# Expert rows added by accumulating scatters onto the base rows and a second tensor, instead of plain scatters into two planes

## The chip, the core and the metric

The kernel runs on one core of a Trainium2 chip. The metric is the device time of one execution in microseconds. A core has TensorE (PE, matmuls), VectorE (DVE), ScalarE (ACT), GpSimd (POOL) and SyncE (SP). SP issues the plain DMAs here, POOL the indirect ones, and 16 DMA engines move the bytes of both.

## What is computed

One layer of a hybrid model on 512 rows of 1024 numbers in f32: a layer norm, a gated delta rule and a differential attention in parallel, a second layer norm, and then a mixture of 16 experts in 4 groups. The change is in that last part:

```
group_prob = softmax(h @ w_rg + b_rg);  g_val, g_idx = top_k(group_prob, 1)
e_prob = softmax(the 4 expert logits of that group);  e_val, e_idx = top_k(e_prob, 2)
e_w = e_val / sum(e_val) * g_val                      # two experts of each row
hid = silu(h @ w_gate[e]) * (h @ w_up[e])             # 1024 -> 256
ffn = sum over the row's two experts of e_w * (hid @ w_down[e])   # 256 -> 1024
ple = sigmoid(h @ w_ple_gate + b) * (p @ w_ple_proj)
out = layer_norm(alpha * h + ffn + ple, ln2_g, ln2_b)
```

## The kernel before

Rows are worked on in four tiles of 128. The part ahead of the experts is long and untouched but for the router. It leaves in DRAM `h1d`, the rows that go into the experts, and `acc`, the base rows (alpha * h plus the ple term, scaled).

**Routing** (`route`, `slots`). `R` holds for each row and each of its two choices one-hot expert, row number and weight. `slots` turns it, with one-hot matmuls, into three tables with a column for each expert: `ts` (which row stands in slot p of the expert, an index out of bounds where the slot is empty), `tw` (its weight) and `td` (twice the row number, plus one where the expert is the row's second choice).

**Experts** (the loop at L1422). For expert e, POOL gathers its rows from `h1d` three experts ahead (L1223), TensorE transposes them (`psx`), `up` makes the gate and up products, `down` the down product, and ScalarE writes the weighted rows to `y` (L1288, two buffers). An indirect DMA of POOL then scatters `y` into `planes` (L1291), a tensor of 2 x 512 rows that was cleared at the start of the kernel (`clear_planes`, L324): each pair of row and choice has its own plane row, so nothing is added in DRAM. Matmuls are made of three products of split operands, and the splits are written by ScalarE (the high part, L265) and VectorE (the low part, L266).

**Weights** come on SP's queue (`load_to`, L246): for each expert two loads `wE` and one `wD`, 1 MB each. From the first expert on, a load waits until the load three before it has landed (`DEEP`, "few loads in flight").

**The last two experts** (14 and 15, `LAST`) aren't scattered: `keep_expert` keeps their weighted rows in SBUF (`ykeep`, high and low part, L1283 and L1284), and `spread` puts them on their rows with one-hot matmuls (`plast`, L1479).

**The end** (`finish`). Base rows are loaded to `at` (L1340) and planes to `pl` (L1345, 1 MB a tile). VectorE adds the planes of tiles 0 to 2 (`add_plane`, L1349, two a tile), TensorE adds those of tile 3 by identity matmuls (L1476). `add_last` adds `plast` and sums the rows (L1486, L1488), ScalarE takes the squares (L1489), `dev` and POOL's power make the deviation (L1492, L209), `norm` scales the rows (L1496), TensorE transposes them (`pzt`), and ScalarE and VectorE write the output pieces (L1518, L1520), which SP stores.

**What sets the order.** Queues are in order. A scheduler orders instructions of the traced program by their dependencies; `strict` keeps the order of writing on an engine within its block, and `behind` puts instructions behind the last one of an engine. A DMA on a DRAM tensor waits for earlier DMAs on the same tensor whose rows may be the same; an indirect one counts as touching all rows. `beyond` works on rows past 128 of an expert, behind a branch.

Of the kernel before, what the change touches and what calls it, by code (L numbers as in the profile page):

```python
# [12 lines left out]
I32 = mybir.dt.int32  # L13
# [59 lines left out]
def block_kernel(ctx, tc, x, pT, wA, wB, wO, wM, wPG, wPP, wE, wD, cols, rows, consts, out):  # L73
# [242 lines left out]
    planes = dp.tile([2 * S, D], F32, name="planes")  # L316
# [3 lines left out]
    def clear_planes():  # L320

        dst = planes.rearrange("(p r) (a b) -> p (r a) b", r=8, b=512)
        for i in range(4):
            nc.sync.dma_start(dst[:, 4 * i:4 * i + 4, :],  # L324
                              nil.rearrange("p (o b) -> p o b", o=1).to_broadcast([128, 4, 512]))
# [770 lines left out]
    def route():  # L1096
# [50 lines left out]
        R = cp.tile([128, 8, 64], F32, name="Rr")  # L1147
        POOL.memset(R[:, 0:4, 48:64], 0.0)
# [7 lines left out]
        DVE.tensor_copy(R[:, 4:8, 48:64], R[:, 4:8, 32:48])  # L1156
# [29 lines left out]
        RT["s"], RT["w"], RT["d"] = slots(0)  # L1186


    def slots(b):
# [5 lines left out]
        for c in range(8):  # L1195
            oh = sp.tile([128, 128], F32, name="oh", tag="oh")
            DVE.tensor_scalar(oh, iota, pos[:, c:c + 1], None, op0=OP.is_equal)
            PE.matmul(pi[:, 0:64], oh, RT["R"][:, c, :], start=c == 0, stop=c == 7)
# [77 lines left out]
    def down(hT, dw, wcol, idxs, mmul, keep=None, y=None, inside=None):  # L1276
# [53 lines left out]
    def finish_expert(e):  # L1330
        down(hTs.pop(e), weights("D", e, loads=ahead(e), splits=SPLITS), ecol("w", e), ecol("d", e), mm3)
# [10 lines left out]
    def load_planes(*tiles):  # L1342
        for t in tiles:
            pl[t] = big([2, 1024], name="pl")
            nc.sync.dma_start(pl[t].rearrange("p c d -> p (c d)"),  # L1345
                              planes[t * 256:(t + 1) * 256, :].rearrange("(p c) d -> p (c d)", c=2))

    def add_plane(t, c):
        DVE.tensor_tensor(at[t // 2][:, t % 2, :], at[t // 2][:, t % 2, :], pl[t][:, c, :], op=OP.add)  # L1349

    def add_planes(*tiles):
        for t in tiles:
            for c in range(2):
                add_plane(t, c)
# [291 lines left out]
```

## Time and profile before

| | |
|---|---|
| median of 3 runs | 671.49 us (670.57 to 672.28) |
| profiled execution | 671.27 us, of which the span is 669.5 us |
| TensorE busy | 650.7 us, 97% of the span |
| VectorE busy | 496.0 us, 74% |
| ScalarE busy | 371.8 us, 56% |
| moved by DMA | 127.17 MB, 190 GB/s in the mean |
| granted TensorE clock | 1.00 to 640 us, 0.87 in the mean from 640 to 670 us |

Times in rows are microseconds from the span's start. A row of a time line gives start, busy time, engine, line, operation, and in brackets how long the engine had been idle and what ended it. SPq and POOLq are the queues that issue DMAs. "out<-in" names the tiles with their numbers left out.

### The profile page before, as it was taken

Reading aid. Unit: us, or ns where it says so; the run is one execution under the profiler, and the core shown is the slowest. Engines: PE = TensorE matmul, PEld = TensorE weight load, DVE = VectorE, ACT = ScalarE, POOL = GpSimd, SP = SyncE. Lnnn points to the kernel's source line nnn. Section 1 sums busy time; section 2 is a strip of 40 time slices with the busy share of each in tenths; the row PEclk is TensorE's granted clock in tenths of the full one; section 3 lists DMA queues with packets and bytes.
Section 4 is the critical chain, followed back from the end, with each engine's and each line's share of the span. In section 5 each row is a group of like instructions: output and inputs, shape, how many; then the busy total and the mean of one; then the engine's idle time right before and its main releaser. Section 6 shows DMA issues by size and latency. Waiting matters only on the chain.

```text
span 669.5 us, 9576 instructions
## 1 busy us (share of the span) xinstructions
PE 650.7 (97%) x3515; PEld 544.3 (81%) x3516; DVE 496.0 (74%) x922; ACT 371.8 (56%) x694; POOL 93.8 (14%) x108
## 2 busy tenths in 40 slices
PE   8999999999998999999999999999999999999993
PEld 4998888888887888888888888899978888888762
DVE  4956678995367684864726284879789999999984
ACT  6707544562466564564523232123379888989734
POOL 2000030100001212200000010200213122221310
PEclk9999999999999999999999999999999999999997
DMA  8994015113103410231611464195489999999553
GB/s 314 404 411 176 1 21 199 63 64 95 64 1 134 141 64 1 69 120 64 251 64 64 137 269 165 64 367 198 162 317 397 378 368 357 359 373 341 187 242 130
DMA packets 31764, 127.17 MB, mean 190 GB/s; under 512 B 9585, under 2 KB 11249, under 8 KB 20576
## 3 DMA queue, kind: packets, MB, share of 16 engines
q1 hardware_dynamic: 27392, 118.73, 47.2%
q0 software_dynamic: 4320, 7.77, 3.2%
q8 instruction: 29, 0.48, 0.3%
q14 instruction: 23, 0.19, 0.1%
HBM read 111.91 MB, written 22.54 MB: 201 GB/s over the span
## 4 chain that ended last, share of the span: by engine, by line
PE 58%; DVE 5%; ACT 3%; issue 1%; POOL 0%; POOLq 0%; ACTq 0%
PE pg L291 12%; PE pg L290 12%; PE pg L289 12%; PE pup L291 3%; PE pup L289 3%; PE pup L290 3%; PE pdn L291 2%; PE pdn L290 2%; PE pdn L289 2%; PE psx L1232 2%; ACT sE L265 1%; PE pov L931 1%; DVE sE L266 1%; DVE sD L266 1%; PE psc L902 1%; ACT xT L1234 1%
## 5 line engine op out<-in xcount | busy, mean ns | idle before, releaser
L289 PE MATMUL pg<-hTh,sA 128*128 128x512 f32 x320 | 129.6, 405 | 0.0
L291 PE MATMUL pg<-hTh,sA 128*128 128x512 f32 x320 | 126.8, 396 | 0.0
L290 PE MATMUL pg<-hTl,sA 128*128 128x512 f32 x320 | 126.5, 395 | 0.0
L266 DVE TENSOR_TENSOR sE<-wE,sE 128x1024 fp32r<-128x1024 f32 x64 | 75.4, 1219 | 0.3 <-ACT sE L265 0.3
L291 PEld LDWEIGHTS pg<-hTh,sA 128*128 128x128 f32 x320 | 60.2, 188 | 13.2
L289 PEld LDWEIGHTS pg<-hTh,sA 128*128 128x128 f32 x320 | 60.3, 188 | 11.5
L290 PEld LDWEIGHTS pg<-hTl,sA 128*128 128x128 f32 x320 | 60.3, 189 | 11.2
L265 ACT ACTIVATE sE<-wE 128x1024 fp32r<-128x1024 f32 x64 | 64.5, 1070 | 0.5 <-PE pg L291 0.4
L265 ACT ACTIVATE sA<-wA 128x1024 fp32r<-128x1024 f32 x40 | 41.4, 1055 | 34.7 <-PE pg L291 31.9
L266 DVE TENSOR_TENSOR sA<-wA,sA 128x1024 fp32r<-128x1024 f32 x40 | 48.7, 1225 | 6.8 <-ACT sA L265 6.6
L289 PE MATMUL pup<-sE,xT 128*128 128x512 f32 x128 | 51.6, 403 | 0.0
L290 PE MATMUL pup<-sE,xT 128*128 128x512 f32 x128 | 50.4, 394 | 0.7 <-DVE sE L266 0.7
L291 PE MATMUL pup<-sE,xT 128*128 128x512 f32 x128 | 50.4, 394 | 0.0
L266 DVE TENSOR_TENSOR sD<-wD,sD 128x1024 fp32r<-128x1024 f32 x32 | 37.8, 1220 | 3.5 <-ACT sD L265 3.3
L290 PE MATMUL pg<-sPG,H1H 128*128 128x262 f32 (+1 forms) x128 | 36.6, 286 | 0.0
L289 PE MATMUL pg<-sPG,H1H 128*128 128x262 f32 (+1 forms) x128 | 36.5, 286 | 0.0
L291 PE MATMUL pg<-sPG,H1L 128*128 128x262 f32 (+1 forms) x128 | 36.5, 285 | 0.0
L265 ACT ACTIVATE sD<-wD 128x1024 fp32r<-128x1024 f32 x32 | 32.5, 1081 | 0.0
L906 ACT ACTIVATE tt<-tt,mn 128x128 f32<-128x128 f32 (+3 forms) x32 | 17.8, 556 | 24.1 <-DVE mn L904 24.0
L1223 POOL DMA_INDIRECT xr<-h1d,ts x16 | 19.1, 1194 | 85.0 <-PE psx L1232 39.9
L530 DVE SCALAR_TENSOR_TENSOR acc<-pad,col,acc 128x512 f32<-128x512 f32 x36 | 26.7, 742 | 3.8 <-ACT acc L528 3.5
L290 PEld LDWEIGHTS pup<-sE,xT 128*128 128x128 f32 x128 | 24.1, 188 | 6.1 <-DVE sE L266 1.2
(369 smaller groups left out, 1528.2 us busy)
## 6 DMA issues: line engine op xcount, KB each, us to landing
wE<-wE SPq DMA_DIRECT2D x32, 1024.0 KB, 9.8
wA<-wA SPq DMA_DIRECT2D x20, 1024.0 KB, 5.0
wD<-wD SPq DMA_DIRECT2D x16, 1024.0 KB, 10.0
wPG<-wPG SPq DMA_DIRECT2D x4, 1048.0 KB, 7.0
planes<-nil SPq DMA_DIRECT2D x4, 1024.0 KB, 11.2
wO<-wO SPq DMA_DIRECT2D x4, 1024.0 KB, 4.8
wM<-wM SPq DMA_DIRECT2D x4, 1024.0 KB, 4.8
pl<-planes SPq DMA_DIRECT2D x4, 1024.0 KB, 10.9
```

What stands on the lines that cost most here:

```text
L265: ACT.activation(hl[:, 0], r, AF.Copy)
L266: lo_eng.tensor_tensor(hl[:, 1], r, hl[:, 0].bitcast(F32), op=OP.subtract)
L289: PE.matmul(ps, lh, rh, start=i == 0, stop=False)
L290: PE.matmul(ps, lh, rl, start=False, stop=False)
L291: PE.matmul(ps, ll, rh, start=False, stop=i == n - 1)
L530: DVE.scalar_tensor_tensor(acc, pad[:, j:j + 512], w[j], acc, op0=OP.mult, op1=OP.add)
L902: PE.matmul(ps[:, :n], qs[:, tq], kl[:, :n], start=False, stop=True)
L906: ACT.activation(tt[:, :n], tt[:, :n], AF.Exp, bias=mn[:, m:m + 1], scale=-1.0, accum_out=(s0[:, qt:qt + 1] if m == 0 else s1))
L931: PE.matmul(po[:, qt * 128:(qt + 1) * 128], aT[:, k * 128:(k + 1) * 128], VB[:, k, vo:vo + 128], start=k == 0, stop=k == qt)
L1223: POOL.indirect_dma_start(out=xr, out_offset=None, in_=h1d, in_offset=bass.IndirectOffsetOnAxis(ap=idx, axis=0), bounds_check=S - 1, oob_i ...
L1232: PE.transpose(ps[:, k * 128:(k + 1) * 128], xr[:, (kk * 4 + k) * 128:(kk * 4 + k + 1) * 128], ident)
L1234: ACT.activation(xT[:, 0, ks, :], h4(ps), AF.Copy)
```

## The change

The planes become one tensor `odd` of 512 rows, cleared at the start by two transfers instead of four. The scatter of an expert adds to its destination (`compute_op=OP.add`): even experts add to `acc`, odd ones to `odd`, at the row number `ts`; the table `td` and what makes it go. The scatters of the loop now alternate between two tensors. At the end `at` is loaded from `acc` behind its scatters, `pl` from `odd` (0.5 MB a tile), and there is one addition a tile, all on VectorE. The additions are at new places: tile 0 ahead of the first `ykeep`, tiles 1 and 2 inside `keep_expert` of experts 14 and 15, tile 3 behind `add_last(0)`. Tile 0's norm goes to ScalarE (`slide`, `norm_act`), `norm(2)` stands ahead of the transposes, and the output pieces are divided otherwise between the two engines.

```diff
--- before.py
+++ after.py
...
-    planes = dp.tile([2 * S, D], F32, name="planes")
+    odd = dp.tile([S, D], F32, name="odd")
...
-        dst = planes.rearrange("(p r) (a b) -> p (r a) b", r=8, b=512)
-        for i in range(4):
+        dst = odd.rearrange("(p r) (a b) -> p (r a) b", r=4, b=512)
+        for i in range(2):
...
-        R = cp.tile([128, 8, 64], F32, name="Rr")
-        POOL.memset(R[:, 0:4, 48:64], 0.0)
+        R = cp.tile([128, 8, 48], F32, name="Rr")
...
-        DVE.tensor_copy(R[:, 4:8, 48:64], R[:, 4:8, 32:48])
...
-            PE.matmul(pi[:, 0:64], oh, RT["R"][:, c, :], start=c == 0, stop=c == 7)
+            PE.matmul(pi[:, 0:48], oh, RT["R"][:, c, :], start=c == 0, stop=c == 7)
...
-        td = cp.tile([128, 16], F32, name=nm("td"))
-        DVE.scalar_tensor_tensor(td, tf, 2.0, pi[:, 48:64], op0=OP.mult, op1=OP.add)
-        td_ = cp.tile([128, 16], I32, name=nm("tdi"))
-        DVE.tensor_copy(td_, td)
-        return ts_, tw, td_
+        return ts_, tw
...
-        POOL.indirect_dma_start(out=planes, out_offset=bass.IndirectOffsetOnAxis(ap=idxs, axis=0), in_=y, in_offset=None,
-                                bounds_check=2 * S - 1, oob_is_err=False)
+        POOL.indirect_dma_start(out=onto, out_offset=bass.IndirectOffsetOnAxis(ap=idxs, axis=0), in_=y, in_offset=None,
+                                bounds_check=S - 1, oob_is_err=False, compute_op=OP.add)
...
-        down(hTs.pop(e), weights("D", e, loads=ahead(e), splits=SPLITS), ecol("w", e), ecol("d", e), mm3)
+        down(hTs.pop(e), weights("D", e, loads=ahead(e), splits=SPLITS), ecol("w", e), ecol("s", e), mm3,
+             onto=(acc, odd)[e % 2])
...
+    def load_planes():
+        pl.update({i: big([2, 1024], name="pl") for i in range(2)})
+        for t in range(NT):
+            nc.sync.dma_start(pl[t // 2][:, t % 2, :], odd[t * 128:(t + 1) * 128, :])
+
+    def add_plane(t):
+        DVE.tensor_tensor(at[t // 2][:, t % 2, :], at[t // 2][:, t % 2, :], pl[t // 2][:, t % 2, :], op=OP.add)
...
         if e == NE - 1:
-            load_planes(2, 3)
             turn_last = late.pop(e)
 
             def between():
                 turn_last()
-                with behind(DVE):
-                    add_plane(0, 0)
-
-            keep_expert(e - 1, inside=between)
+                add_plane(1)
+
+            with behind(DVE), strict(DVE):
+                add_plane(0)
+                keep_expert(e - 1, inside=between)
+                keep_expert(e, inside=partial(add_plane, 2))
...
             load_base()
-            load_planes(0, 1)
-    keep_expert(NE - 1, inside=next_plane)
-    with behind(DVE):
-        add_planes(1)
+            load_planes()
...
-                if t == 3 and add:
-                    for c in range(2):
-                        PE.matmul(ps[-1], ident, pl[t][:, c, nh * 512:(nh + 1) * 512], start=c == 0, stop=False)
...
+        def slide(t):
+            DVE.tensor_tensor(st[t][:, 6:7], st[t][:, 2:3], st[t][:, 5:6], op=OP.mult)
+
+        def norm_act(t):
+            ACT.activation(R_[t], R_[t], AF.Identity, bias=st[t][:, 6:7], scale=st[t][:, 5:6])
...
             s0, s1, s2, s3 = (spread(t) for t in range(NT))
+            with behind(DVE):
+                add_last(0, s0)
             if add:
-                with behind(DVE):
-                    add_planes(2)
-            add_last(0, s0)
+                add_plane(3)
             add_last(1, s1)
             dev(0)
             add_last(2, s2)
-            norm(0)
+            slide(0)
             dev(1)
+            norm_act(0)
             add_last(3, s3)
             norm(1)
             dev(2)
+            norm(2)
             b0, b1 = [], []
             turn(0, b0)
             turn(1, b0)
-            norm(2)
             leave(0, b0, "AAAA", (4, 8))
...
-            leave(0, b0, "....AAVV", (4, 8))
-            leave(1, b1, "VAVVAVAV", (4, 8))
+            leave(0, b0, "....VAVV", (4, 8))
+            leave(1, b1, "AVAVAVAV", (4, 8))
```

On POOL the last scatters before, with the one-hot rows of the kept experts behind them (`y` is the expert's rows, `tdi` the integer table `td`):

```order
L1291 DMA planes<-y_5709,tdi_4344 1024x1024
L1291 DMA planes<-y_5806,tdi_4344 1024x1024
L1291 DMA planes<-y_5881,tdi_4344 1024x1024
L1291 DMA planes<-y_5928,tdi_4344 1024x1024
L1359 TENSOR_SCALAR to_row_5966<-cst,tf_4337 128x128 x4
```

and now:

```order
L1284 DMA acc<-y_5701,ts_4336 512x1024
L1284 DMA odd<-y_5798,ts_4336 512x1024
L1284 DMA acc<-y_5873,ts_4336 512x1024
L1284 DMA odd<-y_5920,ts_4336 512x1024
L1347 TENSOR_SCALAR to_row_5958<-cst,tf_4333 128x128 x4
```

The place in the queue is the same; the destination alternates, so that a scatter shares its tensor with the last but one.

On SP the end of the weight loads and the loads of the last part before:

```order
L246 DMA wD_5838<-wD 128x2048
L1340 DMA at_5991<-acc 128x1024 x2
L1340 DMA at_5992<-acc 128x1024 x2
L1345 DMA pl_5997<-planes 128x2048
L1345 DMA pl_5999<-planes 128x2048
L1345 DMA pl_6077<-planes 128x2048
L1345 DMA pl_6079<-planes 128x2048
```

and now:

```order
L246 DMA wD_5830<-wD 128x2048
L1334 DMA at_5983<-acc 128x1024 x2
L1334 DMA at_5984<-acc 128x1024 x2
L1339 DMA pl_5989<-odd 128x1024 x2
L1339 DMA pl_5990<-odd 128x1024 x2
```

The order stands. The loads of `acc` now come behind scatters into `acc` (the last is expert 12's) and those of `odd` behind expert 13's; half as much is loaded to `pl`.

On VectorE the end before, from the last expert's gate (`eth`) to the first sums of `add_last` (L1486):

```order
L1263 TENSOR_TENSOR eth_6073<-eth_6073,pup_6036 128x256
L1284 SCALAR_TENSOR_TENSOR ykeep_6081<-pdn_6082,tw_4335,ykeep_6081 128x512
L1273 TENSOR_TENSOR hT_6094<-psf_6091,hT_6094 128x256
L1349 TENSOR_TENSOR at_5991<-at_5991,pl_5997 128x1024
L1284 SCALAR_TENSOR_TENSOR ykeep_6081<-pdn_6098,tw_4335,ykeep_6081 128x512
L1284 SCALAR_TENSOR_TENSOR ykeep_6107<-pdn_6108,tw_4335,ykeep_6107 128x512
L1349 TENSOR_TENSOR at_5991<-at_5991,pl_5997 128x1024
L1284 SCALAR_TENSOR_TENSOR ykeep_6107<-pdn_6118,tw_4335,ykeep_6107 128x512
L1349 TENSOR_TENSOR at_5991<-at_5991,pl_5999 128x1024 x2
L1349 TENSOR_TENSOR at_5992<-at_5992,pl_6077 128x1024 x2
L1486 ISA at_5991,st_6129<-plast_6136,at_5991 128x512
```

and now:

```order
L1256 TENSOR_TENSOR eth_6067<-eth_6067,pup_6030 128x256
L1342 TENSOR_TENSOR at_5983<-at_5983,pl_5989 128x1024
L1277 SCALAR_TENSOR_TENSOR ykeep_6072<-pdn_6073,tw_4331,ykeep_6072 128x512
L1266 TENSOR_TENSOR hT_6085<-psf_6082,hT_6085 128x256
L1342 TENSOR_TENSOR at_5983<-at_5983,pl_5989 128x1024
L1277 SCALAR_TENSOR_TENSOR ykeep_6072<-pdn_6089,tw_4331,ykeep_6072 128x512
L1277 SCALAR_TENSOR_TENSOR ykeep_6098<-pdn_6099,tw_4331,ykeep_6098 128x512
L1342 TENSOR_TENSOR at_5984<-at_5984,pl_5990 128x1024
L1277 SCALAR_TENSOR_TENSOR ykeep_6098<-pdn_6109,tw_4331,ykeep_6098 128x512
L1463 ISA at_5983,st_6118<-plast_6125,at_5983 128x512
```

The first addition now stands ahead of the first `ykeep`, and the sums of `add_last` follow the last `ykeep` at once.

## Rows read from the trace of the kernel before

**Rows 1.** The page: busy time of the engines, and TensorE in 40 slices of the span, in tenths.

```profile
PE 650.7 (97%) x3515; PEld 544.3 (81%) x3516; DVE 496.0 (74%) x922; ACT 371.8 (56%) x694; POOL 93.8 (14%) x108
...
PE   8999999999998999999999999999999999999993
```

**Rows 2.** Who TensorE waited for from 480 to 645 us: the longest sum (us in total, times, longest).

```profile
PE pdn L289 <- ACT sD L265: 0.8, 1, 0.8
```

**Rows 3.** The chain of work that ended last, TensorE's transposes of the rows of two experts, nine apart (start, us).

```profile
511.49 0.87 PE psx L1232 x8
...
596.53 0.87 PE psx L1232 x8
```

**Rows 4.** What SP's queue waited for from 500 to 616 us (us in total, times, longest).

```profile
SPq L246 <- DMA wE<-wE: 68.8, 23, 4.1
SPq L246 <- DMA wD<-wD: 32.2, 12, 3.7
```

**Rows 5.** The time line of SP's queue: the pairs of loads of experts 8 and 14, the last two down weights, and the base rows.

```profile
533.31 3.38 SPq L246 DMA_DIRECT2D wE<-wE  x2
...
593.60 4.02 SPq L246 DMA_DIRECT2D wE<-wE  x2
...
610.60 3.71 SPq L246 DMA_DIRECT2D wD<-wD  x2
618.22 2.04 SPq L1340 DMA_DIRECT2D at<-acc  x4
```

**Rows 6.** Two lines of the code in one stretch each: the last load of weights, and the loads of the base rows, with the time from issue to landing.

```profile
L246 SPq DMA_DIRECT2D wD<-wD x1: 327/327/327, 614.0 to 614.0; - x1
...
DMA to landing us min/median/max: 9.2/9.2/9.2
...
L1340 SPq DMA_DIRECT2D at<-acc x4: 320/376/432, 618.2 to 619.8; - x4
...
DMA to landing us min/median/max: 6.2/7.4/8.9
```

**Rows 7.** The time line of ScalarE: the second half of expert 12's rows, the splits of the last two down weights, and the first operation behind them.

```profile
618.23 0.69 ACT L1288 ACTIVATE y<-pdn,tw 128x512 f32<-128x512 f32 x1 [0.71 <-PE pdn L291]
...
628.03 2.04 ACT L265 ACTIVATE sD<-wD 128x1024 fp32r<-128x1024 f32 x2
...
630.29 2.00 ACT L265 ACTIVATE sD<-wD 128x1024 fp32r<-128x1024 f32 x2
634.10 0.38 ACT L1271 ACTIVATE hT<-psf 128x256 fp32r<-128x256 f32 x1 [1.81 <-PE psf L1268]
```

**Rows 8.** The time line of VectorE at the end: gate of the last expert, first and last `ykeep`, plane additions, one `norm`, one `dev`, the last `norm`, output pieces.

```profile
637.07 0.42 DVE L1263 TENSOR_TENSOR eth<-eth,pup 128x256 f32<-128x256 f32 x1
638.32 0.75 DVE L1284 SCALAR_TENSOR_TENSOR ykeep<-pdn,tw,ykeep 128x512 fp32r<-128x512 f32 x1 [0.83 <-ACT ykeep L1283]
...
643.22 0.74 DVE L1284 SCALAR_TENSOR_TENSOR ykeep<-pdn,tw,ykeep 128x512 fp32r<-128x512 f32 x1
643.88 4.87 DVE L1349 TENSOR_TENSOR at<-at,pl 128x1024 f32<-128x1024 f32 x4
...
653.13 0.80 DVE L1496 TENSOR_SCALAR at<-at,st 128x1024 f32<-128x1024 f32 x1
653.85 0.15 DVE L1492 TENSOR_SCALAR st<-st 128x1 f32<-128x1 f32 x1
...
658.44 0.81 DVE L1496 TENSOR_SCALAR at<-at,st 128x1024 f32<-128x1024 f32 x1 [0.66 <-POOL st L209]
659.17 2.35 DVE L1520 TENSOR_SCALAR z<-pzt,col 128x256 f32<-128x256 f32 x5
661.71 1.00 DVE L1520 TENSOR_SCALAR z<-pzt,col 128x256 f32<-128x256 f32 x2 [0.19 <-ACT z L1518]
```

**Rows 9.** Busy time by stretch: stretch, its length, then PE, PEld, DVE, ACT and POOL, the granted clock, the busy share of the 16 DMA engines, and GB/s. The stretches are the router and first experts, one at the start in which only plain DMAs run, two among the experts, and one in which the last scatter runs nearly alone.

```profile
420.00:520.00 100.00, 98.98 (x661) 89.70 (x660) 86.66 (x198) 47.41 (x73) 18.59 (x13) 1.00 0.68 256
...
40.00:50.00 10.00, 10.00 (x84) 9.91 (x83) 3.25 (x9) 1.40 (x4) 0.00 (x0) 1.00 1.05 412
510.00:520.00 10.00, 10.00 (x50) 8.22 (x49) 10.00 (x13) 9.01 (x13) 2.74 (x2) 1.00 1.00 404
540.00:550.00 10.00, 10.00 (x54) 8.32 (x52) 9.63 (x12) 9.08 (x14) 2.17 (x2) 1.00 0.91 343
632.50:633.10 0.60, 0.60 (x5) 0.41 (x3) 0.60 (x2) 0.00 (x0) 0.60 (x1) 1.00 0.28 109
```

**Rows 10.** The time line of POOL: the last three scatters (experts 11 to 13). Then, for the scatters' line, the time from issue to landing over all 14.

```profile
614.12 0.99 POOL L1291 DMA_INDIRECT planes<-y,tdi  x1 [8.48 <-ACT sE L265]
623.58 0.97 POOL L1291 DMA_INDIRECT planes<-y,tdi  x1 [8.47 <-ACT sE L265]
630.39 1.02 POOL L1291 DMA_INDIRECT planes<-y,tdi  x1 [5.84 <-ACT eth L1261]
...
DMA to landing us min/median/max: 3.7/8.7/9.9
```

**Rows 11.** The page: POOL's DMA queue (packets, MB, share of 16 engines), and the indirect DMAs (count, us to landing).

```profile
q0 software_dynamic: 4320, 7.77, 3.2%
...
xr<-h1d,ts POOLq DMA_INDIRECT x16, 8.5
planes<-y,tdi POOLq DMA_INDIRECT x14, 8.7
```

More of the change, by code (lines that the diff above doesn't have):

```diff
@@ L1185, in route @@
         yield 1
-        RT["s"], RT["w"], RT["d"] = slots(0)
+        RT["s"], RT["w"] = slots(0)
     def slots(b):
@@ L1274, in turn_h, with down @@
         return hT
-    def down(hT, dw, wcol, idxs, mmul, keep=None, y=None, inside=None):
+    def down(hT, dw, wcol, idxs, mmul, keep=None, y=None, inside=None, onto=None):
         y = half_slot("y") if keep is None and y is None else y
@@ L1340, in load_base @@
             nc.sync.dma_start(at[t // 2][:, t % 2, :], acc[t * 128:(t + 1) * 128, :])
[L1342 to L1352, printed above, removed]
-            for c in range(2):
-                add_plane(t, c)
+    def load_planes():
[4 more added lines that the diff above has]
+        DVE.tensor_tensor(at[t // 2][:, t % 2, :], at[t // 2][:, t % 2, :], pl[t // 2][:, t % 2, :], op=OP.add)
     def find_rows(e):
@@ L1376, in beyond @@
             wd = dp.tile([3, 128, 16], F32, name="ovw")
-            dd = dp.tile([3, 128, 16], I32, name="ovd")
             for b in range(1, 4):
-                ts_, tw, td = slots(b)
+                ts_, tw = slots(b)
                 nc.sync.dma_start(sd[b - 1], ts_)
                 nc.sync.dma_start(wd[b - 1], tw)
-                nc.sync.dma_start(dd[b - 1], td)
             we = [big([4, 512], name="we") for _ in range(2)]
@@ L1386, in beyond @@
             y = half_slot("y")
-            is_, iw, id_ = tiny(1, "is", I32), tiny(1, "iw"), tiny(1, "id", I32)
+            is_, iw = tiny(1, "is", I32), tiny(1, "iw")
             with tc.For_i(0, NE, 1) as e:
@@ L1393, in beyond @@
                         nc.sync.dma_start(iw, wd[b - 1, :, bass.ds(e, 1)])
-                        nc.sync.dma_start(id_, dd[b - 1, :, bass.ds(e, 1)])
                         for kh in range(2):
@@ L1400, in beyond @@
                         turn_h(th, False, hT)
-                        down(hT, lambda f, sl: (wd_[:, f, sl], None), iw, id_, mm1, y=y)
+                        down(hT, lambda f, sl: (wd_[:, f, sl], None), iw, is_, mm1, y=y, onto=acc)
             load_base()
-            load_planes(*range(NT))
-            add_planes(*range(NT))
+            load_planes()
+            for t in range(NT):
+                add_plane(t)
             finish(False)
@@ L1416, in turn_into @@
             hTs[e] = turn_h(th, True)
-    def next_plane():
-        with behind(DVE):
-            add_plane(0, 1)
     for e in range(NE):
@@ L1457, in block_kernel @@
             load_base()
-            load_planes(0, 1)
-    keep_expert(NE - 1, inside=next_plane)
-    with behind(DVE):
-        add_planes(1)
+            load_planes()
     def finish(add=True):
@@ L1473, in spread @@
                 ps.append((gbank if 2 * t + nh in (4, 5, 6) else bank)("plast"))
-                if t == 3 and add:
-                    for c in range(2):
-                        PE.matmul(ps[-1], ident, pl[t][:, c, nh * 512:(nh + 1) * 512], start=c == 0, stop=False)
                 for e in LAST:
@@ L1479, in spread @@
                         PE.matmul(ps[-1], to_row[e][:, t, :], ykeep[e][:, i, nh * 512:(nh + 1) * 512],
-                                  start=e == LAST[0] and i == 0 and not (t == 3 and add), stop=e == LAST[1] and i == 1)
+                                  start=e == LAST[0] and i == 0, stop=e == LAST[1] and i == 1)
             return ps
@@ L1526, in finish @@
             s0, s1, s2, s3 = (spread(t) for t in range(NT))
+            with behind(DVE):
+                add_last(0, s0)
             if add:
-                with behind(DVE):
-                    add_planes(2)
-            add_last(0, s0)
+                add_plane(3)
             add_last(1, s1)
```

## The prediction

> **What bounds the kernel now.** I read the page first, then the waits of the stretch in which the experts run, then the time lines of its queues, and last the end of the kernel. TensorE is busy for 97% of the span, and the slices show it at 9 tenths in all but the first and the last [rows 1]. In the stretch of the experts it waits for almost nothing: the largest sum is one wait of 0.8 us, for a split weight [rows 2]. One expert takes (596.53 - 511.49)/9 = 9.45 us, read from the rows' transposes that open each [rows 3]. So TensorE sets the pace there, but a second engine runs beside it with less air than that suggests. The DMA queue of SP, which loads the weights, spends 68.8 + 32.2 = 101 us of the 116 us from 500 to 616 waiting for an earlier load to land [rows 4]: three loads are in flight at any time, and none of that waiting is for a free buffer. The load of expert 8's first half was issued at 533.31 and that of expert 14's at 593.60, so weights come at (593.60 - 533.31)/6 = 10.05 us an expert [rows 5], slower than the 9.45 us at which they are used. The kernel lives on the lead that the first loads have. At the end it is nearly gone: the last down weights, issued at 613.99, land 9.2 us later, at 623.2 [rows 6], and ScalarE starts to split them at 630.29 [rows 7]. The cover is 7.1 us, and 1.8 us more of idle ScalarE stands behind that split, before 634.10 [rows 7].
>
> The last part is another regime. From 637 on, VectorE is the chain: behind the last expert's second half (643.22) it adds four plane tiles in 4.87 us from 643.88, and then works on through the adds and norms until the last norm at 658.44, with gaps of no more than 0.7 us [rows 8].
>
> **What the end gains.** Before, six plane tiles are added on VectorE, four of them behind the last `ykeep`, and two more by identity matmuls. Now there are four tiles: one in front of the first `ykeep`, one inside each of the two kept experts, and one between `add_last(0)` and `add_last(1)`. Of the four behind the last `ykeep` three go: 3 x 4.87/4 = 3.65 us [rows 8]; the adds that stand earlier fill waits for ScalarE, 0.8 us and more [rows 8]. The identity matmuls cost nothing before, as TensorE was ahead of VectorE there, and give nothing. `norm(0)` (0.80 us) goes to ScalarE and leaves one 128x1 operation, 0.15 us like `dev` [rows 8]: VectorE gains 0.6 us, but ScalarE does the 1024 columns (1.0 us, as half of its sD pair [rows 7]) before the squares of tile 3, which `norm(3)` waits for; I keep 0.35 us. VectorE has seven output pieces behind `norm(3)` before and after, so nothing changes there. Sum: 4.0 us earlier, if all inputs are there in time.
>
> **What costs nothing.** One copy, one scalar-tensor-tensor and one cast fewer in the router, a memset less, matmuls of 48 columns for 64 and a few rows in another order: TensorE is busy 98.98 of 100 us there [rows 9], and at most its 1.0 us of idling could go. Half of the clearing (2 of 4 MB) goes from 30 to 50 us; TensorE is busy for every microsecond of that stretch too [rows 9], so the freed transfer hides behind it. The scatters' waits become looser. Before, each waits for the one before to land; the starts at 614.12, 623.58 and 630.39, 7 to 9.5 us apart, with a median landing of 8.7 us, are that chain [rows 10]. Now each waits for the last but one, some 19 us back. POOL's next row gather stands behind it, and the longest wait of TensorE, for a split, is 0.8 us [rows 2], so this gives nothing by itself; scatter 12 can start when its rows are written, near 619 [rows 7], and not at 623.58.
>
> **What accumulating costs.** No accumulating transfer is in this trace. What a plain indirect one costs the loads can be read. Loads alone run at 412 GB/s [rows 9], so three of 1.049 MB take 7.64 us. They take 10.05 us where one gather and one scatter an expert run beside them, so the two cost 2.41 us, 1.2 us each. By bytes it should be half: queue 0 moved 7.77 MB in 30 transfers [rows 11], 0.26 MB each, 0.63 us at 412 GB/s. The reason is seen where a scatter runs nearly alone (632.5 to 633.1): the 16 DMA engines are busy to a share of 0.28, four to five of them [rows 9]. Some 64 of 128 rows are real, they stand in the first partitions, and a part of the engines carries them, while a load has landed only when its slowest part has. The slices agree: 404 GB/s in 510 to 520, 343 GB/s in 540 to 550 [rows 9].
>
> An accumulating scatter must read its destination rows and write them. Lower bound of the extra: 0, if the read hides behind the write; less than a plain scatter is excluded, as it writes the same bytes. Upper bound: 2.4 us, a gather and a scatter's worth on top, if reading, adding and writing don't overlap. I take the read as what the nearest row has, a gather of as many rows: x = 1.2 us a scatter.
>
> The Trainium skill (Collectives: The Full Stack, "The bandwidth ceiling: the fold count and why AG ≠ RS ≠ AR") says that a DMA engine that adds has two sources to read in one ring, and got 32.35 GB/s where copying got 62.28. By that ratio, 1.93, the extra would be 0.93 x 1.2 = 1.1 us, an estimate, and the sum below 674.5 us; no accumulating transfer here shows it.
>
> Before the last down weights land there are 13 scatters (0 to 11, and now 12). 13 x 1.2 = 15.6 us, so they land at 623.2 + 15.6 = 638.8 us. That uses up the cover of 7.1 + 1.8 us; TensorE would be 6.7 us late. It isn't the last word. The base rows can now be loaded only when scatter 12 has landed, behind these weights, not at 618.22 [rows 5], and the odd rows behind them in the same queue. The four base loads ended 8.9 us after 619.8 [rows 6], at 628.7, 5.5 us behind the weights' landing; one of 0.5 MB takes about 1.4 us. So the first odd tile lands 5.6 + 1.4 = 7.0 us after the weights: 645.8 us. `add_plane(0)` is now ahead of the first `ykeep` on VectorE, a place reached at 637.5 before [rows 8]; behind it are queued both `ykeep`s, `hT` of the last expert, for which TensorE waits, and all of the end. So 645.8 - 637.5 = 8.3 us late, which contains TensorE's 6.7.
>
> Sum: +8.3 - 4.0 = +4.3 us on the profiled execution's 671.27 us. That stands 0.2 us under the median of the runs, 671.49. Forecast: 675.8 us. In general the change is -4.0 + max(0, 13x - 7.3) us: it breaks even at x = 0.87 us.
>
> **Rivals.** Faster, on the other side: the read of the destination hides. One mechanism, the place is the weight queue from 507 to 623 us, the price is x. Below x = 0.56 nothing of the lead is missed and the end's 4.0 us stand: 667.5 us; up to 0.72 it is still faster by 0.3%. For it: half of the DMA engines have air [rows 9], and the lead is 7.1 us. Against it: the loads wait for the slow half, and the end is no better if the odd rows come late.
>
> In between: x from 0.72 to 1.02 us, lead and gain cancel within 2 us: 671.5 us.
>
> Dearer: read, add and write in turn, x = 2.4. The lead is gone some experts earlier and each expert then takes over 12 us (10.05 + 2.4): -4.0 + 31.2 - 7.3 = +19.9, 691.4 us. For it: the loaded landing is 8.7 us against 3.7 us without load [rows 10], so this queue suffers from company. Against it: a DMA that reads one row while it writes another is what the plain ones do.
>
> **How the numbers follow.** 0.3% is 2.0 us, about what a measurement of this kernel can tell from no change. x above 1.02 us has 0.51 (0.40 up to x = 1.6, 681.0 us; 0.11 above), between 0.72 and 1.02 it has 0.14, below 0.35. So slower 0.51, same 0.14, faster 0.35. The likeliest case alone spans 673.5 to 681.0 us. The range takes in the faster case with 1.2 us of error in the end's sum, 666.3, and reaches up to x = 1.7, 682.0; it leaves out about 0.09 above and 0.08 below.
>
> **What would show it.** Right: weight loads of experts 8 to 14 issued 11 us apart or more, TensorE waiting for splits or splits for landings from expert 11 or 12 on, the last down weights landing near 639 us, VectorE waiting some microseconds before its first plane add, and 4 us fewer from there to the end. Wrong: loads still 10 us apart and no wait of ScalarE for one; then x is near 0, the end's gain is all there is, and the time is near 667.5. Spans of 12 us an expert would show the dear case. If the end from the first `ykeep` on isn't shorter by 3 to 5 us, the other term is wrong.

## The result, and the profile after

The changed kernel takes **680.71 us** (median of 4 runs, 679.96 to 683.27); the kernel before took 671.38 us beside it (4 runs, 670.57 to 672.28). The ratio is 1.0145, 95% interval 1.0114 to 1.0177: 9.3 us slower. The forecast was 675.8 us. The direction came as forecast, the size did not: 9.3 us where 4.3 were forecast. The profiled execution below is the longest of its four, 683.27 us with a span of 681.5; its own difference to the profiled one of before is 12.0 us, and sums read from it are held against 12.0, not against 9.3.

The page first. POOL's queue, which carries the gathers and scatters, moves the bytes it moved before [rows 11] in half as much time again, and waits for DMA are now a good part of the chain that ended last:

```profile
PE 653.1 (96%) x3507; PEld 548.8 (81%) x3508; DVE 493.6 (72%) x917; ACT 373.8 (55%) x695; POOL 101.1 (15%) x107
...
q0 software_dynamic: 4320, 7.78, 4.7%
...
PE 42%; DMA 22%; DVE 2%; issue 2%; ACT 1%; POOL 0%; SPq 0%; POOLq 0%; DVEq 0%; ACTq 0%
```

That chain before:

```profile
PE 58%; DVE 5%; ACT 3%; issue 1%; POOL 0%; POOLq 0%; ACTq 0%
```

4.7% of 681.5 us is 32.0 us of all 16 engines; before, it was 3.2% of 669.5, 21.4 us. The 14 scatters thus cost 10.6 us more, 0.76 us each over 16 engines, or 1.5 us each if half of the engines carry them. The whole queue's mean before was 21.4/30 = 0.71 us a transfer, 1.43 on half of the engines. If a plain scatter costs that mean, an accumulating one costs about twice as much.

The time line of SP's queue, to be read beside [rows 5] (start, us, engine, line, tiles, count):

```profile
537.45 4.14 SPq L246 DMA_DIRECT2D wE<-wE  x2
...
611.16 4.40 SPq L246 DMA_DIRECT2D wE<-wE  x2
...
629.32 2.80 SPq L246 DMA_DIRECT2D wD<-wD  x2
639.71 1.89 SPq L1334 DMA_DIRECT2D at<-acc  x4
```

The loads of experts 8 and 14 are now (611.16 - 537.45)/6 = 12.29 us an expert apart; they were 10.05, and TensorE uses an expert's weights up in 9.45. The lead is lost at expert 10: the split of its second half, on ScalarE's time line, is the first of 15 that wait for a load, and from there on most do. Then follows who ScalarE and TensorE waited for from 480 to 660 us (us in total, times, longest; the first two of these rows are ScalarE's, the others TensorE's):

```profile
580.90 2.01 ACT L265 ACTIVATE sE<-wE 128x1024 fp32r<-128x1024 f32 x2 [1.32 <-DMA wE<-wE]
```

```profile
ACT sE L265 <- DMA wE<-wE: 10.1, 10, 1.5
...
ACT sD L265 <- DMA wD<-wD: 3.6, 5, 1.1
...
PE psf L1261 <- DVE eth L1256: 9.7, 6, 2.1
PE pdn L289 <- DVE ykeep L1277: 2.0, 1, 2.0
```

Before, TensorE's longest sum was 0.8 us [rows 2], and ScalarE waited for no load. What these waits add up to is read at the last down weights, on ScalarE's time line, where [rows 7] had 630.29. The first `ykeep` stands beside it, first before, then, behind the split, now:

```profile
637.60 0.69 ACT L1283 ACTIVATE ykeep<-pdn,tw 128x512 fp32r<-128x512 f32 x1 [1.02 <-PE pdn L291]
```

```profile
642.26 2.00 ACT L265 ACTIVATE sD<-wD 128x1024 fp32r<-128x1024 f32 x2 [0.21 <-DMA wD<-wD]
...
649.09 0.69 ACT L1276 ACTIVATE ykeep<-pdn,tw 128x512 fp32r<-128x512 f32 x1 [1.00 <-PE pdn L291]
```

The split starts 12.0 us late and has just waited for its load, so that load landed at about 642.2, 19.0 us later than before (623.2). TensorE's product, which ScalarE copies as the first `ykeep`, is 11.5 us late. Last, VectorE at the end, beside [rows 8]:

```profile
651.16 1.22 DVE L1342 TENSOR_TENSOR at<-at,pl 128x1024 f32<-128x1024 f32 x1 [2.17 <-DMA pl<-odd]
652.31 0.74 DVE L1277 SCALAR_TENSOR_TENSOR ykeep<-pdn,tw,ykeep 128x512 fp32r<-128x512 f32 x1
...
657.98 0.74 DVE L1277 SCALAR_TENSOR_TENSOR ykeep<-pdn,tw,ykeep 128x512 fp32r<-128x512 f32 x1
658.64 0.68 DVE L1463 CUSTOM_DVE_ANT_0 at<-plast,at 128x512 f32<-128x512 f32 x1
...
668.99 0.81 DVE L1479 TENSOR_SCALAR at<-at,st 128x1024 f32<-128x1024 f32 x1 [0.66 <-POOL st L209]
```

The first plane add waits for the odd rows and starts 13.7 us later than VectorE reached that place before (637.5). From the last `ykeep` to the last `norm` it is now 11.0 us; it was 15.2 (643.22 to 658.44). But the last `ykeep` is 14.8 us late, 3.3 us more than the first on ScalarE. Between the two TensorE waited 2.0 us for VectorE's first `ykeep`, which stands behind the add that waits for the odd rows (the last row of the waits above). Then its clock fell, as the stretches show (columns of [rows 9]), first the kernel before, then two of the changed one:

```profile
654.00:656.00 2.00, 1.08 (x8) 0.84 (x8) 1.96 (x6) 1.00 (x3) 0.55 (x1) 1.00 0.01 4
```

```profile
646.00:648.00 2.00, 2.00 (x11) 1.61 (x10) 0.49 (x2) 0.29 (x1) 2.00 (x4) 1.00 0.86 272
654.00:656.00 2.00, 2.00 (x6) 1.60 (x5) 1.18 (x2) 0.54 (x1) 0.00 (x0) 0.50 0.01 4
```

A granted clock of 0.50 is the lower of its two levels: six matmuls fall into 2 us where eleven did just before.

### The profile page after: what moved, and what is told of

The parts are those of the page before. It is cut to its first block, busy times and chain, and to the rows that moved or that the text cites. A ratio compares the mean times of both kernels' runs of the same rounds, so it can differ in the third digit from the quotient of the medians.

```text
span 681.5 us, 9548 instructions
## 1 busy us (share of the span) xinstructions
PE 653.1 (96%) x3507; PEld 548.8 (81%) x3508; DVE 493.6 (72%) x917; ACT 373.8 (55%) x695; POOL 101.1 (15%) x107
## 4 chain that ended last, share of the span: by engine, by line
PE 42%; DMA 22%; DVE 2%; issue 2%; ACT 1%; POOL 0%; SPq 0%; POOLq 0%; DVEq 0%; ACTq 0%
DMA wE<-wE 18%; PE pg L289 12%; PE pg L291 12%; PE pg L290 12%; DMA odd<-y,ts 3%; PE pov L931 1%; DMA pl<-odd 1%; PE psc L902 1%; PE psc L901 1%; PE pzt L1488 1%; PE pat L919 1%; DVE at L1463 1%; PE psh L388 1%; DVE at L1342 0%; DVE z L1503 0%
## 5 line engine op out<-in xcount | busy, mean ns | idle before, releaser
L265 ACT ACTIVATE sE<-wE 128x1024 fp32r<-128x1024 f32 x64 | 64.6, 1064 | 11.2 <-DMA wE<-wE 10.1
L289 PEld LDWEIGHTS pg<-hTh,sA 128*128 128x128 f32 x320 | 60.4, 189 | 11.4
L290 PEld LDWEIGHTS pg<-hTl,sA 128*128 128x128 f32 x320 | 60.4, 189 | 11.1
L289 PE MATMUL pup<-sE,xT 128*128 128x512 f32 x128 | 52.3, 409 | 0.0
L290 PE MATMUL pup<-sE,xT 128*128 128x512 f32 x128 | 51.2, 400 | 0.7 <-DVE sE L266 0.7
L291 PE MATMUL pup<-sE,xT 128*128 128x512 f32 x128 | 51.0, 398 | 0.0
## 6 DMA issues: line engine op xcount, KB each, us to landing
wE<-wE SPq DMA_DIRECT2D x32, 1024.0 KB, 10.7
```

Of the source, the lines that this page charges most:

```text
L265: ACT.activation(hl[:, 0], r, AF.Copy)
L289: PE.matmul(ps, lh, rh, start=i == 0, stop=False)
L290: PE.matmul(ps, lh, rl, start=False, stop=False)
L291: PE.matmul(ps, ll, rh, start=False, stop=i == n - 1)
```

## The experiments

The theory (A): accumulating itself makes each scatter dearer, the DMA engines that carry it are the ones for which every weight load waits, and the lead runs out. Rivals: the new order of waits and of the tail alone (B); a limit of the loads in flight (W); two accumulating scatters at once (P); the odd rows' wait ahead of the first `ykeep` (O1). Every experiment ran with the kernel before beside it, on the same chip.

**Accumulating taken out.**

```
-  bounds_check=S - 1, oob_is_err=False, compute_op=OP.add)
+  bounds_check=S - 1, oob_is_err=False)
```

The sums of base rows and experts are then left out; queues, waits and sizes stay.

> The changed kernel with plain scatters: they overwrite rows of acc and odd, so the sums of base rows and experts are left out; queues, waits, sizes and the new end are the same. Theory A (the accumulating transfer's longer hold on the DMA engines starves the weight loads): loads of experts 8 to 14 come 10.0 us apart again instead of 12.3, no wait of ScalarE for a load, and what stays is the end's gain, 667 to 670 us. Theory B (the loss is in the new waits: base and odd rows may be loaded only behind the last scatters): the waits are still there, so the time stays above 674 us, with VectorE waiting for the odd rows.

Measured: 669.31 us, ratio 0.9978 (0.9964 to 0.9992). SP's queue, the pairs of experts 8 and 14:

```profile
531.55 3.64 SPq L246 DMA_DIRECT2D wE<-wE  x2
...
594.03 4.38 SPq L246 DMA_DIRECT2D wE<-wE  x2
```

10.41 us an expert instead of 12.29, no wait of ScalarE for a load. (It isn't the 10.05 of before because 7 scatters and 7 gathers start in this stretch, where 6 and 6 did: 62.48 us less 45.84 for 18 loads at 7.64 is 16.6 us over 14 transfers, 1.19 each; before, 60.29 less 45.84 is 14.5 us over 12, 1.20 each. A plain transfer's price is the forecast's.) One argument taken away gives back 11.4 of 680.7 us: B falls as a cause of the loss, and only the end's gain is left.

**Accumulating put into the kernel before,** with its old waits, one tensor of planes and its old tail.

```
-  bounds_check=2 * S - 1, oob_is_err=False)
+  bounds_check=2 * S - 1, oob_is_err=False, compute_op=OP.add)
```

> The kernel before with accumulating scatters into the same cleared planes; the result is the same. Nothing else is changed. Theory A: weights come about 12 us an expert once the lead is used up, and the time is 678 to 685 us (up to 12 us late at the last down weights less nothing gained at the end). Theory B: the base rows are loaded early as before and only the planes wait, so within 2 us of 671.4.

Measured: 694.33 us, ratio 1.0335 (1.031 to 1.036), dearer than the whole change. The reason is on POOL's time line, three scatters in a row:

```profile
568.42 1.59 POOL L1291 DMA_INDIRECT planes<-y,tdi  x1 [7.59 <-ACT y L1288]
579.90 1.59 POOL L1291 DMA_INDIRECT planes<-y,tdi  x1 [7.51 <-ACT y L1288]
591.13 1.59 POOL L1291 DMA_INDIRECT planes<-y,tdi  x1 [7.26 <-ACT y L1288]
```

and in ScalarE's waits from 480 to 670 us:

```profile
ACT y L1288 <- DMA planes<-y,tdi: 25.2, 10, 3.4
```

Each scatter waits for the one before to land, 9.9 to 10.7 us after its issue. (The brackets name ScalarE's `y`, which ends at the same moment: it is the next expert's, written into the buffer that the landed scatter has freed.) So 11.2 to 11.5 us pass from one to the next, more than the 9.45 of an expert, and ScalarE waits for the buffers `y` that they read. Here the chain of scatters is the bound, not the loads, which theory A had not foreseen. The looser waits of two tensors in turn, which I had priced at nothing, are thus worth some 10 us once scatters accumulate: 694.3 less 680.7 is 13.6 us, and about 3 of them are the new tail's. No run has two tensors with the old tail, so the division is an estimate.

**The real rows dealt over all partitions.** Slots 0 to 7 go to partitions 0, 4, ... 28, the next eight to 64, 68, ... 92, and so on, instead of to neighbours; a table of 128 numbers, loaded at the start, takes the place of `iota` where the slot lists are made. The same rows, bytes and sums.

```
-  DVE.tensor_scalar(oh, iota, pos[:, c:c + 1], None, op0=OP.is_equal)
+  DVE.tensor_scalar(oh, slot, pos[:, c:c + 1], None, op0=OP.is_equal)
...
+  n = np.arange(128)
+  at = n % 16 // 8 * 64 + n % 8 * 4 + n // 16 % 4 + n // 64 * 32
+  cst[:, NCST + 512 + at] = n
```

> The changed kernel with the slots of an expert in another order, so that its 24 to 112 real rows are dealt over all 128 partitions instead of the first ones (one table of 128 numbers more). The result is the same. Theory A1 (a part of the DMA engines carries the real rows and the loads wait for that part): the extra of a scatter halves, loads come 9.4 to 9.7 us apart, no wait for loads, 666 to 670 us. Theory A2 (an accumulating transfer costs the loads as much wherever it runs, through the memory or the queue): loads still 12 us apart, 678 to 683 us.

Measured: **668.52 us, ratio 0.9961 (0.9943 to 0.9979)**, 12 us below the changed kernel and below the kernel before. The page's row of POOL's queue, and the pairs of experts 8 and 14 on SP's time line:

```profile
q0 software_dynamic: 4320, 7.78, 4.8%
```

```profile
530.37 3.65 SPq L247 DMA_DIRECT2D wE<-wE  x2
...
587.10 3.46 SPq L247 DMA_DIRECT2D wE<-wE  x2
```

The scatters cost the engines as much as before the dealing (4.8% of 666.6 us, 32.0 us), and yet the loads come at 9.46 us an expert, which is TensorE's pace. The stretch from 580 to 590 us shows it best (the columns of [rows 9]): first the changed kernel, then the spread one.

```profile
580.00:590.00 10.00, 10.00 (x50) 8.23 (x49) 7.17 (x8) 7.55 (x11) 2.83 (x3) 1.00 0.84 284
```

```profile
580.00:590.00 10.00, 10.00 (x50) 8.21 (x49) 9.63 (x13) 9.12 (x14) 2.78 (x2) 1.00 1.02 379
```

With neighbouring slots the 16 engines are busy to 0.84 while loads are late, which fits a part that idles and a part that is the bound; no view shows the engines one by one. Spread, all are busy (1.02), and they move 379 GB/s instead of 284. POOL takes as long to issue an accumulating scatter as before the dealing (medians of 1.6 to 1.8 us; 1.2 in the plain run), so its longer issue is not the cause of the late loads. The Trainium skill (DMA: Bandwidth & Descriptors, "The descriptor swizzle") gives the map that the dealing follows, for one transfer of 1 MiB to 128 partitions: engines 0 to 7 serve partitions 0 to 63, and each takes groups of four partitions. The spread run agrees with it (9.46 us an expert instead of 12.29).

**The same dealing in the kernel before.**

> The kernel before with the slots dealt over all partitions, as a control of the above. The result is the same. A1: loads of experts 8 to 14 come 9.4 to 9.6 us apart instead of 10.05 (then paced by the use of weights), the cover of the last down weights grows from 7 us to over 10 us, and the time stays at 671 us within 1 us, since TensorE sets the pace and never waited. A2: loads 10.05 us apart as before.

Measured: 670.47 us, ratio 0.9994 (0.9984 to 1.0004). The loads gain here as well (9.46 us an expert instead of 10.05), but nobody had waited for them.

**Five loads in flight.**

```
-  DEEP, FIRST = 3, 0
+  DEEP, FIRST = 5, 0
```

> The changed kernel with five weight loads in flight instead of three. Theory A1 (a load lands when the part of the DMA engines that also carries the scatters has done its share, and that part is never idle): no change, 679 to 683 us, weight loads still 12 us an expert in experts 8 to 14. Rival W (the limit of three in flight leaves engines idle while a scatter runs): the loads run ahead, 10 to 10.5 us an expert, and 668 to 672 us.

Measured: 681.33 us, ratio 1.0159 (1.0142 to 1.0176); experts 8 and 14 are (602.26 - 530.11)/6 = 12.03 us apart. More loads in flight start earlier, and the time is no better: rival W, which wanted 668 to 672 us, falls.

**Only even experts accumulate.** The odd ones write plainly, so where a row has two odd experts one is left out of the sum.

```
-  onto=(acc, odd)[e % 2])
+  onto=(acc, odd)[e % 2], op=(OP.add, OP.bypass)[e % 2])
```

(`down` hands `op` on as the scatter's `compute_op`.)

> The changed kernel with only the even experts' scatters accumulating; the odd ones write plainly onto the second tensor, so where a row has two odd experts one of the two is left out of the sum. Theory L (each accumulating scatter costs the loads about 1.46 us, by itself): 7 of the 13 that precede the last down weights, so these land at 623.2 + 10.2 = 633.4 us, the cover of 8.9 us is passed by 1.3 us, and the run takes 670 to 673 us; weight loads 11.2 us an expert. Rival P (the cost comes from two accumulating scatters in flight at once): these pairs are gone, loads 10.4 us an expert, last down weights before 628, 669 to 670 us.

Measured: 673.03 us (10 runs), ratio 1.0028 (1.0017 to 1.004). Loads 11.42 us an expert; ScalarE splits the last down weights from 633.23, so they had landed by then: at most 10.0 us later than before, at most 1.4 us for each of the 7 accumulating scatters ahead of them. Rival P, which wanted loads 10.4 us apart and 669 to 670 us, falls: no two accumulating ones follow each other here, and the loads are late all the same.

**The changed kernel again,** for a second profile.

> The changed kernel once more, unchanged, for a second profile. Its first profiled execution (683.3 us) was the longest of its four. If that profile speaks for the others: the last down weights are split from 641 to 643 us, the first plane add starts 12 to 14 us later than in the kernel before, and the median is 680 to 682 us. If it was an outlier: split near 639 us, and the add 10 us late.

Measured: 680.72 us, ratio 1.0139 (1.0122 to 1.0156), and the profiled run is again the longest, 685.29. Last down weights split from 643.13, first plane add at 653.29, 15.8 us late: the first profile's terms come back, somewhat larger, in another long run. What lengthens just these two runs, by 2.6 and 4.6 us against their medians, stays open.

**The first plane adds moved behind the first kept expert,** to test O1.

```
-  add_plane(1)
...
-  add_plane(0)
   keep_expert(e - 1, inside=between)
-  keep_expert(e, inside=partial(add_plane, 2))
+  keep_expert(e, inside=partial(steps, map(add_plane, range(3))))
```

> The changed kernel with the first two plane adds moved behind the first kept expert: none ahead of or inside it, three inside the second one. In the changed kernel's profile ScalarE had written the first ykeep half by 649.8 us and VectorE took it at 652.31, behind the add that waits for the odd rows (651.16). Theory O1 (the odd rows' landing holds ykeep, hT and TensorE): the first ykeep starts 2 us earlier, and the run takes 678.5 to 680.0 us. Theory O2 (the late weights alone set the end, the add's wait is hidden beside them): 680.5 to 681.5 us, the last ykeep no earlier.

Measured: 681.28 us, ratio 1.0145 (1.0127 to 1.0164): no gain. VectorE's time line shows why:

```profile
650.36 0.75 DVE L1277 SCALAR_TENSOR_TENSOR ykeep<-pdn,tw,ykeep 128x512 fp32r<-128x512 f32 x1 [0.82 <-ACT ykeep L1276]
...
654.12 3.48 DVE L1342 TENSOR_TENSOR at<-at,pl 128x1024 f32<-128x1024 f32 x3
657.52 0.74 DVE L1277 SCALAR_TENSOR_TENSOR ykeep<-pdn,tw,ykeep 128x512 fp32r<-128x512 f32 x1
```

The first `ykeep` does start 2 us earlier, but the last one starts at 657.52 instead of 657.98, since the three adds now stand in a row ahead of it. `ykeep` itself is 12.0 us late (638.32 before) with nothing of the odd rows in front of it: the weights alone make that. So this move doesn't pay. It doesn't show that the odd rows cost nothing, as the third `ykeep` on ScalarE tells, first before, then in the changed kernel, then here:

```profile
640.70 0.69 ACT L1283 ACTIVATE ykeep<-pdn,tw 128x512 fp32r<-128x512 f32 x1 [0.80 <-PE pdn L291]
```

```profile
655.46 0.69 ACT L1276 ACTIVATE ykeep<-pdn,tw 128x512 fp32r<-128x512 f32 x1 [4.07 <-PE pdn L291]
```

```profile
652.73 0.69 ACT L1276 ACTIVATE ykeep<-pdn,tw 128x512 fp32r<-128x512 f32 x1 [0.80 <-DVE ykeep L1277]
```

It is 14.8 us late with the add in front and 12.0 us late without. The move took these 2.7 us away and lost them again to its own three adds (3.48 us). Whether another place for the adds would keep them no run tells: O1 is neither shown nor refuted as a cost of the time.

**The spread kernel with its first add moved,** and both once more side by side.

```
   def between():
       turn_last()
+      add_plane(0)
       add_plane(1)
...
-  add_plane(0)
```

> The changed kernel with the slots dealt over all partitions, and the first plane add moved from ahead of the first kept expert's ykeep to inside that expert, next to the second add. Theory E1 (the add ahead of the first ykeep delays ykeep, hT and with them TensorE): the last ykeep starts at about 643.2 us instead of 643.87 and the run takes 667.5 to 668.2 us, 0.5 to 1 us less than with the add in front (668.52). Theory E2 (VectorE is the chain from there on, so four adds cost the same wherever they stand): 668.3 to 668.9 us, the last ykeep still at 643.8 or later.

> The changed kernel with spread slots again, beside the next one on the same chip, to size what the add ahead of the first ykeep costs. Both theories: 668.2 to 669.0 us; the last ykeep starts near 643.9 us.

> The same with the first plane add inside the first kept expert. Theory E1 (the add in front, which also waits for the odd rows, delays ykeep): 0.4 to 1.0 us under the spread kernel beside it, with intervals that hardly overlap. Theory E2 (VectorE is the chain, place of the adds without effect): within 0.3 us of it.

Measured: 667.79 us, ratio 0.9953 (0.9939 to 0.9967) for the moved add; side by side 667.32 us, 0.9943 (0.9924 to 0.9962) with the add in front, and 667.58 us, 0.9951 (0.9934 to 0.9967) with it moved. The place of the add makes no difference that can be measured; the gain that the first pair seemed to show is gone in the second.

**Spread slots, plain scatters** (again without the sums).

> The changed kernel with the slots dealt over all partitions and plain scatters in place of accumulating ones (the sums of several experts on one row are left out). Theory A1 (with the rows spread, what accumulating adds to the queue is hidden altogether): the same time as with spread accumulating scatters, 668.0 to 669.0 us, loads 9.45 us an expert. If accumulating still costs something there (a longer landing of scatter 13 ahead of the odd rows' loads): 666.5 to 667.5 us, with the odd rows' loads issued 1 us or more before 634.4.

Measured: 667.79 us, ratio 0.9956 (0.9942 to 0.9970), not to be told from the spread accumulating kernel. In the profile the odd rows' loads start at 630.19 instead of 634.41, and the add in front at 636.22 instead of 637.69; of that the two medians, 667.8 and 668.5 or 667.3, show nothing. Once the rows are spread, what accumulating adds is hidden in the time.

## Why the prediction was right in its way and wrong in its size

**The bound and the mechanism: right.** I had read that the loads live on a lead, that a part of the DMA engines carries the scatters, and that accumulating would use the lead up. The plain run shows that accumulating does it, the spread run that the partitions of the rows decide, and the waits above that the lead runs out. The edits priced at nothing before expert 8 cost nothing: in both kernels ScalarE splits that expert's first weights at the same time (555.93 before, 556.31 now).

**The step that failed first: "I take the read as what the nearest row has, a gather of as many rows: x = 1.2 us a scatter".** In the profiled execution accumulating cost the loads about 1.5 us a scatter on top of a plain one's price, not 1.2. By the last down weights' landing x is 19.0/13 = 1.46 us, a little too much, as scatter 13 was issued at 638.04, ahead of that landing. In the run with 7 accumulating scatters it is at most 1.4, by POOL's queue on half of the engines 1.5. By the loads themselves it comes out so: in the changed kernel, one line of the code in the stretch between the loads of experts 8 and 14 (537 to 611 us; ns min/median/max, first and last start), the scatters and then the gathers:

```profile
L1284 POOL DMA_INDIRECT acc<-y,ts x4: 1587/1650/1774, 545.1 to 607.7; - x4
L1284 POOL DMA_INDIRECT odd<-y,ts x3: 1650/1726/1738, 554.6 to 595.2; - x3
...
L1216 POOL DMA_INDIRECT xr<-h1d,ts x7: 1038/1038/1041, 541.4 to 599.8; - x7
```

73.71 us, less 45.84 for 18 loads and 14 x 1.2 for the transfers as if plain, leaves 11.1 us over 7 scatters: 1.6 us each. A gather was the nearest row, but the wrong one to stop at, as nothing in it adds. The Trainium skill (Collectives: The Full Stack, "The bandwidth ceiling: the fold count and why AG ≠ RS ≠ AR") has a ratio of 1.93 for adding, from which I had estimated 1.1 us; by POOL's queue the ratio is (0.71 + 0.76)/0.71 = 2.07 and by the loads (1.2 + 1.6)/1.2 = 2.3, somewhat dearer than the page. The weights land at 642.2 instead of the 638.8 of the forecast. Error: 3.4 us.

**"So the first odd tile lands 5.6 + 1.4 = 7.0 us after the weights".** That add starts at 651.16, 9.0 us after them. The base rows' and the odd rows' loads, one line of the code each (first and last start; us from issue to landing, min/median/max):

```profile
L1334 SPq DMA_DIRECT2D at<-acc x4: 326/460/497, 639.7 to 641.1; - x4
...
DMA to landing us min/median/max: 6.2/7.5/8.7
```

```profile
L1339 SPq DMA_DIRECT2D pl<-odd x4: 319/404/432, 645.4 to 646.7; - x4
...
DMA to landing us min/median/max: 5.7/6.1/6.6
```

The last base rows, issued at 641.1, land 8.7 us later, at 649.8: 7.6 us behind the weights, not 5.6. The first odd tile, issued at 645.38, lands 5.7 us later, at 651.1: 1.3 us behind the base rows, as forecast. The diff says one wait more, which the forecast left out: the odd rows' loads wait for scatter 13. It was issued at 638.04 and took 7.3 us, beside weights and base rows (before, nearly alone, 3.7 [rows 10]), and so kept these loads back until 645.38. In this execution that was still ahead of the base rows' landing. How much of the 2.0 us is that scatter's, in flight beside the base rows, and how much their later issue, no run separates. Error: 2.0 us.

**"Sum: 4.0 us earlier" from the first plane add on.** In the changed kernel it is 1.7 us: the first add is 13.7 us late and the span ends 12.0 us late. With the weights out of the way the gain is 3.1 us: in the first spread profile the first add starts 0.2 us late and the span ends 2.9 us early (666.6 against 669.5). The last `norm` starts 3.6 us earlier there (654.87 against 658.44), but the add in front of `ykeep` pushes the last `ykeep` from 643.22 to 643.87, and 0.7 us go behind the last `norm`. `norm(0)` takes 1.23 us on ScalarE where I had counted 1.0. The other 1.4 us are lost in the late kernel alone, where TensorE's clock falls to the lower level: from 654 to 656 us, as shown above, and again in the transposes of the end, first the changed kernel, then the spread one:

```profile
666.92 5.38 PE L1488 MATMUL pzt<-cst,at 128*128 128x128 f32 x32 [2.05 <-ACT at L1476]
```

```profile
652.81 4.02 PE L1490 MATMUL pzt<-cst,at 128*128 128x128 f32 x32 [2.04 <-ACT at L1478]
```

The granted clock was 0.50 from 668 to 670 us in the first, 1.00 throughout in the second. The forecast had no term for the clock. That the clock makes up all of the 1.4 us is read from these rows and not tested. Error: 2.3 us.

**The sum again, in the forecast's own terms.**

| us | forecast | profiled execution |
|---|---|---|
| weights land later | 13 x 1.2 = 15.6 | 19.0 |
| first plane add behind them | 7.0 | 9.0 |
| less the place before, 637.5 - 623.2 | -14.3 | -14.3 |
| from there to the end | -4.0 | -1.7 |
| sum | +4.3 | +12.0 |

The path that the sum takes, through the odd rows to the first plane add, is the one that VectorE's rows show: that add waits 2.2 us for them. What it costs beyond the weights' own lateness the moved adds have not settled. All three sizes were short, by 3.4, 2.0 and 2.3 us, 7.7 together. How the 5.0 us between forecast and medians (9.3 against 4.3) divide is not shown: all three profiled executions with this kernel's scatters and three loads in flight (683.27, 685.29 and 683.32 us) were the longest of theirs. The nearest usual one has five in flight, 680.42 us with a span of 678.6. ScalarE's split of its last down weights and VectorE's first plane add:

```profile
639.93 2.00 ACT L265 ACTIVATE sD<-wD 128x1024 fp32r<-128x1024 f32 x2
```

```profile
649.21 1.23 DVE L1342 TENSOR_TENSOR at<-at,pl 128x1024 f32<-128x1024 f32 x1 [2.51 <-DMA pl<-odd]
```

That split waits for no load, so the weights had landed by 639.93, at most 16.7 us later than before: x is at most 1.3 there. The add is 11.7 us late and the span ends 9.1 us late. Of its 4.8 us over the forecast at most 1.1 are the scatters' price; at least 2.3 lie between the weights and the first add, and 1.4 behind it. That the forecast failed by its sizes is shown; which size weighs most in a usual execution stays open.

**"That uses up the cover of 7.1 + 1.8 us".** This stands beside the sum, not in it, but it was wrong too: only the 7.1 us were cover. The load landed 19.0 us late, and the split starts 12.0 late. The 1.8 us of idle ScalarE behind that split were a wait for TensorE, which itself moves with the weights; 0.5 of them were taken up (TensorE's product is 11.5 us late). One reading was loose as well: TensorE is at 8 tenths in the thirteenth slice too [rows 1]; nothing rests on it.

**Fewer accumulating scatters.** The general form, -4.0 + max(0, 13x - 7.3), with 7 for 13 and x = 1.4 gives -1.5 us; measured +2.0 (673.03 against 671.04). The weights are hardly late there (split from 633.23, 2.9 us), and the odd rows are what VectorE waits for: its first add starts at 641.93, 4.4 us behind 637.5.

**The rivals.** The hidden read (x near 0) is refuted for neighbouring slots; with the rows spread the extra is hidden, though by other means than the forecast had, and the time forecast for that case, 667.5 us, is near what the spread runs took (668.52 and 667.32). The dear one, x = 2.4, is refuted by every measure of x, although the loads were 12.29 us an expert apart, and 12 I had given as its mark. The mark was wrong: TensorE keeps its pace while the lead lasts, so in a longer interval of loads more scatters and gathers start (7 and 7 in six experts' loads, above, instead of 6 and 6), and 12 us is reached at x = 1.6 already.

## What to carry to other kernels

A DMA queue that has a lead is on the path with a threshold: find what each added transfer costs it per step, multiply, and subtract the lead alone, not the idle gaps of engines that wait on the delayed work. Then follow what is queued behind it: here the base and odd rows stood 9.0 us behind the weights, and the engine that waited for them stopped TensorE, whose clock then fell. Count the transfers in a stretch, not one per step, and price an indirect one by what it takes of the engines that its real rows reach, not by its bytes. Where only the first partitions hold rows, dealing them over all partitions is worth a try first: here it cost one small table and turned a loss of 9.3 us into a gain of about 3, though it gave the kernel before nothing, as nobody waited for its loads. And where scatters accumulate into one tensor, a wait from each to the one before can become a chain of its own; with two targets in turn the scatters here started ahead of the landing of the one before.

## What the runs showed of the hardware that was not expected

An accumulating scatter took the DMA engines about twice a plain one's time (POOL's queue from 21.4 to 32.0 us, with 14 of 30 transfers accumulating). With the same bytes and the same queue time, the loads came 12.29 us an expert apart when the rows stood in neighbouring partitions and 9.46, TensorE's pace, when they were spread. Three or five loads in flight made no difference that helped (12.29 and 12.03 us an expert, 680.7 and 681.3 us). And TensorE, after a wait of 2.0 us for VectorE, ran at a granted clock of 0.50 from 654 to 656 us, where it had 1.00 before the change.
